# Three layer norms of a transposed encoder trunk: the variance is summed onto all partitions by one wide product, and root and reciprocal run at full width

## The chip, the cores and the metric

The kernel runs on one core of a Trainium2 chip. A core has five engines with queues of their own: TensorE (PE; its weight loads are listed as PEld), VectorE (DVE), ScalarE (ACT), GpSimd (POOL) and SyncE (SP, which only issues DMAs). The metric is the device time of one execution in microseconds, as the median of several runs; one more execution was profiled. Times inside the trace are microseconds from the start of the span, the stretch from the first to the last instruction.

## The reference

A two-layer encoder with width 1024 runs over two request groups, 256 and 512 tokens, each with 16 meta tokens in front (800 token columns in all). Layer 0 mixes tokens by latent attention, layer 1 by windowed grouped-query attention. After the mixer and after the squared-ReLU MLP of each layer stands a residual sum and a layer norm, so there are four norms:

```python
def layer_norm(x, g, b):
    xf = x.astype(jnp.float32)
    mu = jnp.mean(xf, axis=-1, keepdims=True)
    xc = xf - mu
    var = jnp.mean(xc * xc, axis=-1, keepdims=True)
    y = xc * lax.rsqrt(var + LN_EPS) * g.astype(jnp.float32) + b.astype(jnp.float32)
    return y.astype(x.dtype)
...
        h = layer_norm(DN_ALPHA * h + mix, ln1_g[i], ln1_b[i])
        h = layer_norm(DN_ALPHA * h + sqrelu_mlp(h, mlp_w1[i], mlp_w2[i]), ln2_g[i], ln2_b[i])
```

## The kernel before, in words

**Layout.** Activations lie transposed: the 1024 features are 8 chunks of 128 partitions, and the tokens run along the free axis. The 800 columns are two halves of 400 (`hf` 0 and 1); from layer 1's attention on, 384 columns of each half are left (`META` = 16 are dropped). The residual stream is `acc[:, hf, o]`, with o the feature chunk. Every matrix product is taken three times (`mm3`, lines 556 to 558): each operand is split into a rounded part and a rest, the rounding by ScalarE and the rest by VectorE (line 893 or 1661 for activations, 907 or 1624 for weights).

**A layer norm in this layout** sums over partitions, so TensorE does that. For one half (function `layer_norm` at 915 for the attention stages, at 1696 inside the MLP):

- `mean`: a sum over the eight chunks, kept up earlier by POOL and VectorE, is multiplied by `part`, a 128x128 tile of 1/1024 (line 924 or 1708). The result is the mean on every partition, in a PSUM bank `pm`. VectorE subtracts it from each chunk (927, 1710), ScalarE squares (929, 1712), VectorE and POOL add the squares up to one tile v (933 and 935, 1716 and 1718).
- `sums`: v is the stationary operand, in groups of 100 or 128 tokens, against one column of ones (942, 1725). Each product gives one PSUM column, with tokens on partitions. ScalarE takes the root of 100x4 or 128x3 values (946, 1728), VectorE the reciprocal (947, 1729).
- `scale`: TensorE spreads these few values over all partitions again (952, 1734: the column, broadcast, times the identity) into a bank `rb`. VectorE multiplies each chunk by it (957, 1739), ScalarE applies gain and bias (960, 1742), and the result is split for the next products.

Norms over single halves occur as: a0 (layer 0's first norm, half 0, at the end of the attention stage), the one inside the first MLP (the same norm, half 1), b0 and b1 (layer 0's second norm), c0 (layer 1's first norm, half 0), and the one inside the second MLP (half 1). The last norm works by tokens and has another form.

**Around the MLP's norm.** The MLP stage starts with products of half 0 alone (`head_pair`: a first product over chunks 0 to 3, which ScalarE copies out of its bank at line 1828, then a second one over chunks 4 to 7 into the same bank). They stand around `mean`, `sums` and `scale` of half 1. `right_operands` (1759) then makes differences of halves and chunks (line 1767) and splits them (1660, 1661) into the tiles `t` and `h`, which the next products read. The MLP multiplies by a scheme with fewer block products than the plain one, so VectorE and POOL add many blocks.

**Order.** Each of the four stages (attention 0, MLP 0, attention 1 with the end of MLP 0, MLP 1) is a `Plan`: a list of tasks, each with its engine, an entry for its duration in ns, what it reads and writes, and which buffers it takes. TensorE's order in a stage is written out by hand in `ORDERS`, as ranks of its tasks in the order in which the code makes them. For the other engines `forward` picks from the ready tasks by the entries and by due times counted back from the end. The instructions are then issued in that order, and each engine works off its queue in order.

Of the kernel before, what the change touches and what calls it, by code (L numbers as in the profile page):

```python
# [13 lines left out]
F32 = mybir.dt.float32  # L14
# [458 lines left out]
def tile_encoder(ctx: ExitStack, tc: tile.TileContext, ins: dict, y):  # L473
# [410 lines left out]
    def steps(plan):  # L884


        def new(tag, make=None):
            return plan.held(tag, make)
# [26 lines left out]
        def layer_norm(nm, hf, z, n, gi, bi, ss, out, name, tag, st=(), ends=(), root=()):  # L915

            pm, sb, rb = (new("w") for _ in range(3))
# [19 lines left out]
            def sums():  # L937
                v = vs[0]

                def run():  # L940
                    for i in range(n // g):
                        nc.tensor.matmul(sb.t[:g, i : i + 1], v.t[:, i * g : (i + 1) * g], ones, start=True, stop=True)

                plan.task("PE", 645, run, kind="T", reads=[v], writes=[sb], new=[sb], ends=ends)
                m = n // g
                plan.task("ACT", 300, lambda: S.activation(rst[:g, :m], sb.t[:g, :m], AF.Sqrt, bias=eps_ln[:g], scale=1.0 / D), reads=[sb, *root], writes=[("rst", nm)])
                plan.task("DVE", 170, lambda: V.reciprocal(rst[:g, :m], rst[:g, :m]), reads=[("rst", nm)], writes=[("rst", nm)])

            def scale():
                def run():  # L950
                    for i in range(n // g):
                        nc.tensor.matmul(rb.t[:, i * g : (i + 1) * g], rst[:g, i : i + 1].to_broadcast([g, P]), ident[:g, :g], start=True, stop=True)

                plan.task("PE", 800, run, kind="T", reads=[("rst", nm)], writes=[rb], new=[rb])
                for o in range(8):
                    key = ("acc", hf, o)
                    plan.task("DVE", DVE(n), lambda o=o: V.tensor_tensor(z[:, o], z[:, o], rb.t[:, :n], ALU.mult), reads=[rb, key], writes=[key])
                    plan.task(
                        "ACT", 370 + 0.835 * n,
                        lambda o=o: S.activation(z[:, o], z[:, o], AF.Identity, bias=gb[:, bi, o : o + 1], scale=gb[:, gi, o : o + 1]),  # L960
                        reads=[key], writes=[key],
                    )
                    split_to(lambda o=o: out(o), lambda o=o: z[:, o], (name, hf, o), [key, *st], n)
# [82 lines left out]
    def attention0():  # L1046
# [481 lines left out]
        mean, sums, scale = layer_norm("a0", 0, acc[:, 0], HALF, 0, 1, lambda: a0["ss"], lambda o: (a0["h"][0][:, 0, o], a0["h"][1][:, 0, o]), "h", "sqa", [st2], root=["root"])  # L1528
# [25 lines left out]
    def mlp_middle(mp, sqp, late_sum, T, n, l, tiles, yt=None, txs=None, ends=None):  # L1554
# [141 lines left out]
        def layer_norm():  # L1696
# [4 lines left out]
            pm, st, rb = (bank(f"{x}{l}") for x in ("pm", "st", "rb"))  # L1701
            vs = [tmp(f"v{l}{i}") for i in range(2)]
            rst = mp.tile([P, 4], F32, tag="rst", name=f"rst{l}", bufs=1)
            g = 100 if n == HALF else P
            m = n // g
# [14 lines left out]
            def sums():  # L1720
                v = vs[0]

                def run():
                    for i in range(m):
                        nc.tensor.matmul(st.t[:g, i : i + 1], v.t[:, i * g : (i + 1) * g], ones, start=True, stop=True)

                plan.task("PE", 645, run, kind="T", reads=[v], writes=[st], new=[st])
                plan.task("ACT", 400, lambda: S.activation(rst[:g, :m], st.t[:g, :m], AF.Sqrt, bias=eps_ln[:g], scale=1.0 / D), reads=[st], writes=["rst"])
                plan.task("DVE", 170, lambda: V.reciprocal(rst[:g, :m], rst[:g, :m]), reads=["rst"], writes=["rst"])

            def scale():
                def run():
                    for i in range(m):
                        nc.tensor.matmul(rb.t[:, i * g : (i + 1) * g], rst[:g, i : i + 1].to_broadcast([g, P]), ident[:g, :g], start=True, stop=True)

                plan.task("PE", 800, run, kind="T", reads=["rst"], writes=[rb], new=[rb])
                for o in range(8):
                    key = ("acc", 1, o)
                    plan.task("DVE", 570, lambda o=o: V.tensor_tensor(z[:, o], z[:, o], rb.t[:, :n], ALU.mult), reads=[rb, key], writes=[key])
                    plan.task(  # L1740
                        "ACT", 390 + 0.82 * n,
                        lambda o=o: S.activation(z[:, o], z[:, o], AF.Identity, bias=gb[:, bi, o : o + 1], scale=gb[:, gi, o : o + 1]),
                        reads=[key], writes=[key],
                    )
                    if o > 3:
                        split_in(h, (slice(None), 1, o), z[:, o], ("h", 1, o), [key])
# [1175 lines left out]
```

## Time and profile before

| what | us |
|---|---|
| median of 3 runs | 1713.18 (1713.09 to 1713.53) |
| the profiled execution, its own time | 1715.05 |
| its span | 1713.3 |
| TensorE busy | 1695.9 (99%) |
| VectorE busy | 1446.3 (84%) |
| ScalarE busy | 1019.7 (60%) |
| POOL busy | 321.8 (19%) |
| DMA moved | 179.32 MB, mean 105 GB/s |

A row of the timeline gives start, duration, engine, line, operation, output<-inputs, shape and count, and in brackets the idle time before it with what ended it. Matmuls are pipelined and their records overlap, so the price of one is read from start to start, not from its own duration. An fp32 product is recorded as two matmuls.

### The profile page before, as it was taken

The page shows a single profiled execution, that of the slowest core. Times are in us where ns is not written, and L with a number is a line of the kernel's source. Part 1 is how long each engine was busy: PE and PEld are TensorE (multiplying, and loading weights), DVE is VectorE, ACT ScalarE, POOL GpSimd, SP SyncE. Part 2 cuts the span into 40 slices and gives each one's busy share as a digit, 9 for nine tenths or more (in the row PEclk, how much of TensorE's full clock was granted, in tenths as well). Part 3 has the DMA queues.
Part 4 walks back from the last instruction along what each step waited for, and adds up shares of the span by engine and source line. Part 5 has one row for each costly group of instructions (what it writes and reads, how often), then busy time and mean ns, then how long its engine had stood idle before and what let it go on. Part 6 is the DMA issues. An engine that isn't in the chain of part 4 may idle for free.

```text
span 1713.3 us, 28343 instructions
## 1 busy us (share of the span) xinstructions
PE 1695.9 (99%) x10468; PEld 1583.0 (92%) x10468; DVE 1446.3 (84%) x2883; ACT 1019.7 (60%) x2132; POOL 321.8 (19%) x373
## 2 busy tenths in 40 slices
PE   9999999999999999999999999999999999999998
PEld 8998988889999999999999998889998888988996
DVE  7787777876889999989886978976888999998877
ACT  6587777773685455545644637775685445544652
POOL 1243333433100111000002332332100212000100
PEclk9999999999999999999999999999999999999999
DMA  6115534447554332222223321111464232222121
GB/s 233 61 43 128 130 87 111 114 129 214 168 202 158 102 113 72 87 74 74 62 62 106 103 66 66 51 50 51 153 209 156 90 123 82 76 86 74 50 99 74
DMA packets 62763, 179.32 MB, mean 105 GB/s; under 512 B 7456, under 2 KB 24992, under 8 KB 59424
## 3 DMA queue, kind: packets, MB, share of 16 engines
q1 hardware_dynamic: 58608, 151.95, 27.4%
q0 software_dynamic: 3584, 25.17, 6.2%
q8 instruction: 82, 1.34, 0.3%
q14 instruction: 57, 0.47, 0.1%
q10 hardware_dynamic: 432, 0.39, 0.1%
HBM read 167.92 MB, written 34.73 MB: 118 GB/s over the span
## 4 chain that ended last, share of the span: by engine, by line
PE 92%; DVE 6%; ACT 1%; issue 0%; DMA 0%; POOL 0%; ACTq 0%; DVEq 0%; POOLq 0%
PE w L558 17%; PE w L556 17%; PE w L557 17%; PE wb L556 4%; PE wb L557 4%; PE wb L558 4%; PE wa L556 3%; PE wa L558 3%; PE wa L557 3%; PE wa L1350 2%; PE wa L1317 2%; PE sa L556 2%; PE sa L558 2%; PE sa L557 2%; PE wb L2620 2%; PE wb L2602 2%
## 5 line engine op out<-in xcount | busy, mean ns | idle before, releaser
L2064 DVE TENSOR_TENSOR acc<-acc,w 128x400 f32<-128x400 f32 (+1 forms) x327 | 195.7, 614 | 16.7 <-PE w L558 15.4
L556 PE MATMUL w<-h,wsp 128*128 128x400 f32 x320 | 110.8, 346 | 1.7 <-ACT sq L1828 1.0
L557 PE MATMUL w<-h,wsp 128*128 128x400 f32 x320 | 110.3, 345 | 0.0
L558 PE MATMUL w<-h,wsp 128*128 128x400 f32 x320 | 110.1, 344 | 0.0
L1661 DVE TENSOR_TENSOR h<-sq,h 128x384 fp32r<-128x384 f32 (+1 forms) x163 | 96.9, 606 | 12.3 <-ACT h L1661 11.6
L1671 POOL TENSOR_TENSOR sq<-sq,sq 128x384 f32<-128x384 f32 (+1 forms) x28 | 33.7, 1207 | 380.8 <-DVE h L1661 182.4
L1661 ACT CAST h<-sq 128x384 fp32r<-128x384 f32 (+1 forms) x163 | 82.8, 518 | 36.7 <-DVE sq L1671 14.5
L558 PE MATMUL w<-h,wspi 128*128 128x400 f32 x280 | 96.6, 345 | 0.3 <-DVE wspi L1624 0.3
L557 PE MATMUL w<-h,wspi 128*128 128x400 f32 x280 | 96.6, 345 | 0.0
L556 PE MATMUL w<-h,wspi 128*128 128x400 f32 x280 | 96.4, 344 | 0.0
L1259 ACT ACTIVATE p<-sa,nm,rq 106x528 f32<-106x528 f32 (+1 forms) x80 | 63.5, 795 | 33.3 <-DVE nm L1256 27.0
L1837 ACT ACTIVATE sq<-sq 128x400 f32<-128x400 f32 (+1 forms) x84 | 44.5, 530 | 53.4 <-DVE sq L1833 52.7
L1833 DVE TENSOR_TENSOR sq<-sq,w 128x400 f32<-128x400 f32 (+1 forms) x97 | 54.2, 559 | 24.4 <-PE w L558 18.4
L556 PE MATMUL w<-t,wspi 128*128 128x400 f32 (+1 forms) x208 | 70.9, 341 | 0.6 <-DVE sq L1833 0.6
L556 PE MATMUL w<-wsp,h 128*128 128x512 f32 (+1 forms) x182 | 71.6, 393 | 0.0
L558 PE MATMUL w<-wsp,h 128*128 128x512 f32 (+1 forms) x182 | 71.5, 393 | 0.0
L557 PE MATMUL w<-wsp,h 128*128 128x512 f32 (+1 forms) x182 | 71.5, 393 | 0.0
L558 PE MATMUL w<-t,wspi 128*128 128x400 f32 (+1 forms) x208 | 70.9, 341 | 0.0
L557 PE MATMUL w<-t,wspi 128*128 128x400 f32 (+1 forms) x208 | 70.8, 341 | 0.0
L1286 POOL TENSOR_TENSOR p<-p,rs 106x512 f32<-106x512 f32 (+1 forms) x40 | 42.7, 1067 | 124.7 <-DVE pk L1277 67.8
L557 PE MATMUL w<-wspi,h 128*128 128x512 f32 (+1 forms) x164 | 64.5, 393 | 0.0
L556 PE MATMUL w<-wspi,h 128*128 128x512 f32 (+1 forms) x164 | 64.4, 393 | 0.0
(846 smaller groups left out, 6034.4 us busy)
## 6 DMA issues: line engine op xcount, KB each, us to landing
wrawo<-in_w_o_dram SPq DMA_DIRECT2D x32, 512.0 KB, 3.6
wraw0d<-in_w2b_dram SPq DMA_DIRECT2D x27, 512.0 KB, 3.5
us<-in_w1q_dram POOLq DMA_DIRECT2D x12, 1024.0 KB, 8.4
wraw1d<-in_w2b_dram SPq DMA_DIRECT2D x21, 512.0 KB, 3.5
ds<-in_w2q_dram POOLq DMA_DIRECT2D x12, 512.0 KB, 5.4
sq<-kept SPq DMA_DIRECT2D x26, 200.0 KB, 3.4
sq<-kept SPq DMA_DIRECT2D x26, 192.0 KB, 3.2
us<-us POOLq DMA_DIRECT2D x4, 1024.0 KB, 5.0
```

What stands on the lines that cost most here:

```text
L556: first = nc.tensor.matmul(out, lh, rh, start=start, stop=False, **kw)
L557: nc.tensor.matmul(out, lh, rl, start=False, stop=False, **kw)
L558: last = nc.tensor.matmul(out, ll, rh, start=False, stop=stop, **kw)
L1259: lambda: S.activation(P_().rearrange("p (a b) -> p a b", b=264), v(), AF.Exp, bias=nm.t[:qm, 0:1], scale=sc, accum_out=rs.t[:qm, 0:1]),
L1286: f = lambda row=row, r=r, w=w: G.tensor_tensor(row()[:, META:T], row()[:, META:T], r().to_broadcast([qm, w]), ALU.mult)
L1317: nc.tensor.transpose(ps.t[:, k * qm : (k + 1) * qm], src[k], ident[:qm, :qm])
L1350: nc.tensor.matmul(av[64 * e : 64 * e + 64, :n], vt.t[:, k, h0 + 64 * e : h0 + 64 * e + 64], PT.t[:, e, k, :n], start=k == 0, stop=False, ...
L1661: return lambda: S.copy(hi(), view()), lambda: V.tensor_tensor(lo(), view(), hi().bitcast(F32), ALU.subtract)
L1833: plan.task("DVE", 570, lambda: V.tensor_tensor(d.t[:, :n], d.t[:, :n], ps.t[:, :n], ALU.add), reads=[ps, d], writes=[d])
L1837: plan.task("ACT", 510, lambda: S.activation(d.t[:, :n], d.t[:, :n], AF.Relu, scale=scale), reads=[d], writes=[d])
L2064: f = lambda: V.tensor_tensor(z, z, ps.t[:, : z.shape[-1]], op)
L2602: nc.tensor.transpose(ps.t[:, n * P : (n + 1) * P], SM.t[:, a : a + P], ident)
```

## The change

Three norms get a new form: a0 and the two inside the MLPs. In `sums`, v is now the moving operand against `part`, the tile of 1/1024 that the mean already uses. One product of full width leaves the variance on all 128 partitions, in one PSUM bank. The root and the reciprocal run in place in that bank over 128x400 (128x384 in the second MLP), and VectorE multiplies the chunks by it. The spreading products, their bank and the small tile `rst` are gone from these norms. b0, b1 and c0 keep the old form.

TensorE's order is written anew for three stages (attention 0, MLP 0, MLP 1); attention 1 keeps its own. Each of the three has one task fewer, the spreading, so ranks behind it drop by one. Beyond that, 34 of the 369 tasks of attention 0, 23 of 350 of MLP 0 and 30 of 320 of MLP 1 stand elsewhere, by at most nine places, and they are spread over the stages. In a0 `sums` stands one product step earlier. In MLP 0 the second product of head 0 is finished before that of head 1, and the products around `sums` and `scale` are turned; in MLP 1 the first twelve places are the same.

```diff
@@ attention 0: its end
-    "287 285 289 294 293 296 298 292 291 295 301 304 299 297 305-306 309 300 302 310 303 312 314 313 307 317 308 311 318 316 319 315 "
-    "320 322 324-326 323 327 321 329 331 328 332 330 333-337 339-346 338 354 349 347-348 350-351 358 355 362-363 352 359 353 360 "
-    "356-357 364 361 365-369",
...
+    "318 324 322 325-326 323 329 327 321 331 328 332 330 333-337 339-346 338 353 347-350 357 354 361 351 362 358-359 352 355-356 363 "
+    "360 364-368",
@@ MLP 0: its beginning
-    "0-4 7-8 5 9-12 6 13-17 19 21 20 22 18 23 25-30 35 31-34 24 36-41 43 46 45 42 47-48 50 49 44 52 51 56 53-55 57 60 58 61 59 62 69 "
+    "0-4 7 5-6 9 8 10 12 11 13-14 16 15 18 20 19 21 17 24-25 22 26-29 34 30-31 23 32-33 35-40 42 45 44 41 46-47 49 48 43 51 55 52-54 50"
@@ MLP 1: its beginning
-    "0-5 7 6 8-14 21 19 15 20 16 22 17-18 23-25 27-29 36 30 26 31 33 32 34 41 40 38 37 42 39 35 49 45 43-44 50-51 48 47 52 46 53-54 57 "
+    "0-5 7 6 8-13 20 18 14 19 15 22-23 21 16-17 24 26-27 25 28-30 32 38 31 33 35 39 37 36 43 40-41 34 45 47-48 42 49-51 44 46 52-53 56 "
...
-        def layer_norm(nm, hf, z, n, gi, bi, ss, out, name, tag, st=(), ends=(), root=()):
-
-            pm, sb, rb = (new("w") for _ in range(3))
+        def layer_norm(nm, hf, z, n, gi, bi, ss, out, name, tag, st=(), ends=(), root=(), wide=False):
+
+            pm, sb = new("w"), new("w")
+            rb = sb if wide else new("w")
...
+                if wide:
+                    plan.task("PE", 765, lambda: nc.tensor.matmul(sb.t[:, :n], part, v.t[:, :n], start=True, stop=True), reads=[v], writes=[sb], new=[sb], ends=ends)
+                    plan.task("ACT", ACT(n), lambda: S.activation(sb.t[:, :n], sb.t[:, :n], AF.Sqrt, bias=eps_ln, scale=1.0), reads=[sb, *root], writes=[(sb, "sd")])
+                    plan.task("DVE", 2570, lambda: V.reciprocal(sb.t[:, :n], sb.t[:, :n]), reads=[(sb, "sd")], writes=[(sb, "r")])
+                    return
...
-                plan.task("PE", 800, run, kind="T", reads=[("rst", nm)], writes=[rb], new=[rb])
+                if not wide:
+                    plan.task("PE", 800, run, kind="T", reads=[("rst", nm)], writes=[rb], new=[rb])
+                by = (rb, "r") if wide else rb
...
-                    plan.task("DVE", DVE(n), lambda o=o: V.tensor_tensor(z[:, o], z[:, o], rb.t[:, :n], ALU.mult), reads=[rb, key], writes=[key])
+                    plan.task("DVE", DVE(n), lambda o=o: V.tensor_tensor(z[:, o], z[:, o], rb.t[:, :n], ALU.mult), reads=[by, key], writes=[key])
...
-        mean, sums, scale = layer_norm("a0", 0, acc[:, 0], HALF, 0, 1, lambda: a0["ss"], lambda o: (a0["h"][0][:, 0, o], a0["h"][1][:, 0, o]), "h", "sqa", [st2], root=["root"])
+        mean, sums, scale = layer_norm("a0", 0, acc[:, 0], HALF, 0, 1, lambda: a0["ss"], lambda o: (a0["h"][0][:, 0, o], a0["h"][1][:, 0, o]), "h", "sqa", [st2], root=["root"], wide=True)
...
             def sums():
                 v = vs[0]
-
-                def run():
-                    for i in range(m):
-                        nc.tensor.matmul(st.t[:g, i : i + 1], v.t[:, i * g : (i + 1) * g], ones, start=True, stop=True)
-
-                plan.task("PE", 645, run, kind="T", reads=[v], writes=[st], new=[st])
-                plan.task("ACT", 400, lambda: S.activation(rst[:g, :m], st.t[:g, :m], AF.Sqrt, bias=eps_ln[:g], scale=1.0 / D), reads=[st], writes=["rst"])
-                plan.task("DVE", 170, lambda: V.reciprocal(rst[:g, :m], rst[:g, :m]), reads=["rst"], writes=["rst"])
+                plan.task("PE", 765, lambda: nc.tensor.matmul(st.t[:, :n], part, v.t[:, :n], start=True, stop=True), reads=[v], writes=[st], new=[st])
+                plan.task("ACT", 530, lambda: S.activation(st.t[:, :n], st.t[:, :n], AF.Sqrt, bias=eps_ln, scale=1.0), reads=[st], writes=[(st, "sd")])
+                plan.task("DVE", 2570, lambda: V.reciprocal(st.t[:, :n], st.t[:, :n]), reads=[(st, "sd")], writes=[(st, "r")])
 
             def scale():
-                def run():
-                    for i in range(m):
-                        nc.tensor.matmul(rb.t[:, i * g : (i + 1) * g], rst[:g, i : i + 1].to_broadcast([g, P]), ident[:g, :g], start=True, stop=True)
-
-                plan.task("PE", 800, run, kind="T", reads=["rst"], writes=[rb], new=[rb])
                 for o in range(8):
                     key = ("acc", 1, o)
-                    plan.task("DVE", 570, lambda o=o: V.tensor_tensor(z[:, o], z[:, o], rb.t[:, :n], ALU.mult), reads=[rb, key], writes=[key])
+                    plan.task("DVE", 570, lambda o=o: V.tensor_tensor(z[:, o], z[:, o], st.t[:, :n], ALU.mult), reads=[(st, "r"), key], writes=[key])
```

The numbers in the tasks (765, 530, 2570) are the planner's own entries in ns, by which it lays out the queues.

More of the change, by code (lines that the diff above doesn't have):

```diff
@@ L1700, in layer_norm @@
             total = plan.held("sq", None, late_sum)
-            pm, st, rb = (bank(f"{x}{l}") for x in ("pm", "st", "rb"))
+            pm, st = (bank(f"{x}{l}") for x in ("pm", "st"))
             vs = [tmp(f"v{l}{i}") for i in range(2)]
-            rst = mp.tile([P, 4], F32, tag="rst", name=f"rst{l}", bufs=1)
-            g = 100 if n == HALF else P
-            m = n // g
             def mean():
```

41 rows, old and new, of the table ORDERS are left out of this document.

## The prediction

> **What bounds the kernel now.** I read the page first: busy shares, then the chain that ended last.
>
> ```profile
> span 1713.3 us, 28343 instructions
> PE 1695.9 (99%) x10468; PEld 1583.0 (92%) x10468; DVE 1446.3 (84%) x2883; ACT 1019.7 (60%) x2132; POOL 321.8 (19%) x373
> PE 92%; DVE 6%; ACT 1%; issue 0%; DMA 0%; POOL 0%; ACTq 0%; DVEq 0%; POOLq 0%
> ```
>
> TensorE (PE) is the bound: 99% busy and 92% of the chain. VectorE (DVE) is second with 6%. So a microsecond that leaves TensorE's queue is a microsecond of the span, as long as what TensorE reads next is there in time. Which stages have no such reserve is seen in the busy time by stage (columns: stretch, its length, then PE, PEld, DVE, ACT, POOL busy with instruction counts, granted clock, DMA share, GB/s) and in the list of waits (total us, times, longest).
>
> ```profile
> 447.00:460.00 13.00, 11.87 (x65) 10.55 (x64) 11.56 (x19) 8.61 (x16) 2.11 (x2) 1.00 0.26 88
> 460.00:560.00 100.00, 100.00 (x554) 100.00 (x553) 88.60 (x152) 67.45 (x126) 3.46 (x2) 1.00 0.55 181
> 560.00:640.00 80.00, 78.90 (x430) 77.82 (x429) 79.08 (x130) 38.80 (x65) 11.59 (x7) 1.00 0.37 112
> 1219.00:1230.00 11.00, 9.67 (x52) 8.46 (x51) 9.24 (x17) 7.05 (x13) 2.04 (x2) 1.00 0.24 85
> PE w L556 <- ACT sq L1828: 2.1, 4, 0.8
> ```
>
> The two MLP norms begin in the stretches at 447 and 1219. TensorE idles 1.13 and 1.33 us there, nearly all of it in four waits (2.1 us) for ScalarE copies out of PSUM (L1828) that sit between the norm's squares. From 460 to 560 TensorE never idles while DVE has 11.4 us free; from 560 to 640 DVE is full. The second row also gives the price of one ordinary 400-wide product: 100 us / 554 = 0.18 us from start to start (0.173 at 384 wide, by width).
>
> **What is removed and added on TensorE.** The variance's column products (L942, L1725) and the spreading products (L952, L1734) each stand between 400- or 384-wide products, so their price is the interval from the last ordinary start before them to the second one after, less two ordinary steps. First the attention stage's norm a0, with its mean product (L924), which has exactly the form of the new wide product: the tile of 1/1024 times 128x400.
>
> ```profile
> 412.57 0.34 PE L558 MATMUL wa<-o,wsp 128*128 128x400 f32 x1
> 412.76 0.83 PE L924 MATMUL wa<-ssum,part 128*128 128x400 f32 x2
> 413.61 0.34 PE L557 MATMUL wa<-o,wsp 128*128 128x400 f32 x1
> ...
> 424.18 0.34 PE L558 MATMUL wa<-o,wspi 128*128 128x400 f32 x1
> 424.36 0.79 PE L942 MATMUL wa<-ones,sqa 128*100 128x1 f32 x8
> 425.28 0.34 PE L557 MATMUL sa<-o,wspi 128*128 128x400 f32 x1
> ...
> 426.01 0.35 PE L558 MATMUL sa<-o,wspi 128*128 128x400 f32 x1
> 426.20 1.03 PE L952 MATMUL wa<-ident,rsta 100*128 100x100 f32 x8
> 427.28 0.35 PE L557 MATMUL wa<-o,wspi 128*128 128x400 f32 x1
> ```
>
> Wide product: 413.61 - 412.57 - 0.36 = 0.68 us. Column products: 425.28 - 424.18 - 0.36 = 0.74. Spreading: 427.28 - 426.01 - 0.36 = 0.91. So a0 saves 0.74 + 0.91 - 0.68 = **0.97 us** of TensorE. Nearly all of it is the spreading; one wide product is hardly cheaper than four narrow ones. The first MLP's norm has the same forms and durations, and I give it the same 0.97; the second MLP's has three column groups and width 384:
>
> ```profile
> 457.06 0.79 PE L1725 MATMUL w<-ones,sq 128*100 128x1 f32 x8
> 459.99 1.03 PE L1734 MATMUL w<-ident,rst 100*128 100x100 f32 x8
> ```
>
> ```profile
> 1230.32 0.34 PE L558 MATMUL w<-hc,wsp 128*128 128x384 f32 x1
> 1230.49 0.72 PE L1725 MATMUL w<-ones,sq 128*128 128x1 f32 x6
> 1231.34 0.34 PE L557 MATMUL w<-hc,wspi 128*128 128x384 f32 x1
> ...
> 1233.08 0.34 PE L558 MATMUL w<-hc,wspi 128*128 128x384 f32 x1
> 1233.25 0.83 PE L1734 MATMUL w<-ident,rst 128*128 128x128 f32 x6
> 1234.10 0.34 PE L557 MATMUL w<-hc,wsp 128*128 128x384 f32 x1
> ```
>
> Columns 1.02 - 0.35 = 0.67, spreading 0.67, wide product 0.68 x 384/400 = 0.65: **0.69 us** saved. Sum on TensorE: 0.97 + 0.97 + 0.69 = **2.63 us**.
>
> **What is added on ScalarE and VectorE.** The root goes from 100x4 to the full width, in place in PSUM; a 400-wide ScalarE pass out of PSUM is in the trace (L1828).
>
> ```profile
> 457.60 0.51 ACT L1828 ACTIVATE sq<-w 128x400 f32<-128x400 f32 x1
> 458.00 0.26 ACT L1728 ACTIVATE rst<-w,eps_ln 100x4 f32<-100x4 f32 x1
> ```
>
> So 0.25 us more, three times, on an engine 60% busy: nothing on the path beyond the latency counted below. A wide reciprocal stands nowhere in the trace; the nearest rows have one and four columns (min/median/max ns).
>
> ```profile
> L1262 DVE RECIPROCAL rs<-rs x80: 144/164/166, 108.0 to 377.6; 106x1 f32<-106x1 f32 x64, 104x1 f32<-104x1 f32 x16
> L2553 DVE RECIPROCAL rs<-rs x24: 168/178/179, 1039.1 to 1165.2; 128x4 f32<-128x4 f32 x24
> ```
>
> Medians: 14 ns for three more columns, 4.7; I take 5 ns a column, 0.16 + 400 x 0.005 = 2.16 us (2.08 at 384). Ends: below, no dearer than an ordinary pass over PSUM, 0.53 us (two in 1.05 us, the 461.06 row below); above, longest four against shortest one, 35/3 = 11.7 ns a column, 4.8 us. I stay at the middle because both medians rest on many rows.
>
> [...]
>
> **Where it lies.** In the first MLP, DVE is queued like this around the root:
>
> ```profile
> 456.21 2.35 DVE L1624 TENSOR_TENSOR wspi<-wraw0f,wspi 128x1024 fp32r<-128x1024 f32 x2
> 458.48 0.17 DVE L1729 RECIPROCAL rst<-rst 100x4 f32<-100x4 f32 x1
> 458.57 1.20 DVE L1624 TENSOR_TENSOR wsp<-wraw0f,wsp 128x1024 fp32r<-128x1024 f32 x1
> 461.06 1.05 DVE L1739 TENSOR_TENSOR acc<-acc,w 128x400 f32<-128x400 f32 x2 [1.30 <-PE w L1734]
> ```
>
> The multiplications (L1739) waited 1.30 us for the spreading product, which TensorE's order puts at 459.99 although the small reciprocal was done at 458.65. Now: wide product 457.06 to 457.74, root from 457.9 to 458.4, reciprocal to about 460.7, multiplications from 460.8: no later than before. What is late is the weight split (L1624) that the reciprocal pushes behind it and everything after: 2.16 - 0.17 - 1.30 = 0.69 us. The same for the second MLP (idle 0.76): 2.08 - 0.18 - 0.76 = 1.14 us. Who waits? The first tight reader is TensorE's first product with the right-hand sums t (L1661), whose last quarter reads the last t:
>
> ```profile
> 488.21 0.56 DVE L1661 TENSOR_TENSOR t<-tsum,t 128x400 fp32r<-128x400 f32 x1
> 492.04 0.34 PE L556 MATMUL w<-t,wspi 128*128 128x400 f32 x1
> ...
> 1234.12 1.48 DVE L1739 TENSOR_TENSOR acc<-acc,w 128x384 f32<-128x384 f32 x3 [0.76 <-PE w L1734]
> ...
> 1260.80 1.06 DVE L1661 TENSOR_TENSOR t<-tsum,t 128x384 fp32r<-128x384 f32 x1 [0.23 <-ACT t L1661]
> 1265.15 0.34 PE L556 MATMUL w<-t,wsp 128*128 128x384 f32 x1
> ```
>
> Room: 492.04 - 488.77 = 3.27 us and 1265.15 - 1261.86 = 3.29 us. TensorE now comes 0.97 and 0.69 us sooner, DVE 0.69 and 1.14 later: 1.61 and 1.46 us stay. So the reciprocal costs nothing on the path; without that cover, each microsecond of lateness would cost one. The lateness itself is gone before the full stretch at 560, since DVE has 11.4 us free before it.
>
> In a0 the summing task also moves one product step ahead (1.10 us):
>
> ```profile
> 422.38 0.57 DVE L1436 SCALAR_TENSOR_TENSOR acc<-xr,wa 128x400 f32<-128x400 f32 x1 [1.03 <-PE wa L558]
> 422.86 0.57 DVE L935 TENSOR_TENSOR sqa<-sqa,sqa 128x400 f32<-128x400 f32 x1
> ```
>
> It would start at 423.26, before its operand (L935, done 423.43). Either DVE takes L935 ahead of L1436, for which it idled 1.03 us, or TensorE waits some 0.2 us; I take nothing. The half that this norm makes is read by the MLP stage at 447; its eight multiplications, at 0.53 us each behind the spreading product at 426.20, are done by about 432, so 15 us of other products hide its reciprocal. Behind it in DVE's queue stand evacuations and one weight split.
>
> **The new orders** add and drop no other TensorE task: 34 of 369, 23 of 350 and 30 of 320 tasks stand elsewhere, by nine places at most. The other engines' queues, SP's and POOL's DMA issues among them, are laid out anew around that, with the same issues. I take zero, with ends from the waits row: 2.1 us gained if those four waits go, 2.1 lost if as many come. One bank is held longer (the variance's, until the last multiplication) and one is not taken any more; no wait of today is for a bank at these places other than those four.
>
> **Sum.** The profiled execution took 1715.05 us, 1.75 around its span of 1713.3; less 2.63 it would be 1712.42. It ran 1.87 above the median of the runs, 1713.18, so against the median: 1710.55, and I say **1710.5 us**, 0.15% faster. What a measurement of this kernel can tell from no change is about 0.2%, 3.4 us: 1709.75 and 1716.6 are the borders.
>
> **Rivals.**
> *The orders also take standing waits away.* For it: the first MLP's line changes exactly at its two waits (1.0 of the 2.1 us). Against: the first twelve places of the second MLP's line are the old ones. First MLP's alone 1709.5, all four 1708.4; about 1709.0.
> *Late operands.* The reciprocal at its upper end, 4.8 us: lateness 3.33 and 3.66 us against 2.30 and 2.60 of room, so 1.0 + 1.1 us come back: 1712.6. For it: DVE is over 88% busy there. Against: the slope of the small rows.
> *The gain is given back.* DVE is full from 560 to 640; if it sets the pace there, TensorE only arrives earlier and waits: 1713.2. Against: DVE idles before that stretch, waiting for TensorE, so it moves forward with it.
> *Slower.* The reciprocal stands in DVE's queue ahead of a weight split or evacuation that TensorE needs next, and TensorE stands for its whole length at all three norms: 2.16 + 2.16 + 2.08 = 6.4, less 2.63: 1717.0. It decides from 0.9 us of wait per norm on. For it: the first MLP's new line begins its fourth head product one step after the third instead of three, so that weight's split is needed earlier. Against: both splits (456.21, two in 2.35 us) fit before the root.
>
> **Numbers.** Forecast 0.52 (its own range 1709.7 to 1711.5: a wait of 0.2 us here or there, readings of a few hundredths each), waits removed 0.28, late operands 0.09, given back 0.04, slower 0.07. Faster by over 0.2%: the second case and a sliver of the first, 0.32; slower 0.07; within, 0.61. The range goes from all waits gone, 1708.4, to the gain given back, 1713.3, and leaves out the slower case and some of the tails.
>
> **What would show it.** Right: no spreading products at the three places, one wide product of 0.68 us each, reciprocal rows of about 2.2 us, the 1.30 and 0.76 us of DVE idle before the multiplications gone, no TensorE wait for t. Wrong: a TensorE wait for a DVE t, h or weight row between 455 and 495 or 1230 and 1270; a reciprocal above 3.5 us; or savings that come from rows far from the norms.

## The result, and the profile after

| | before | after |
|---|---|---|
| median of 6 runs each, us | 1713.43 (1713.09 to 1715.27) | 1705.26 (1704.34 to 1706.25) |
| profiled execution, its own time, us | 1715.05 | 1706.25 |
| span, us | 1713.3 | 1704.5 |
| TensorE busy, us | 1695.9 | 1686.4 |

The ratio is 0.995, with a 95% interval from 0.9937 to 0.9962: 8.2 us less, where 2.6 were forecast. The time lies below the range. The page of the profile after, its first lines and the engines' shares of the chain:

```profile
span 1704.5 us, 28243 instructions
PE 1686.4 (99%) x10430; PEld 1576.8 (93%) x10430; DVE 1452.2 (85%) x2888; ACT 1019.8 (60%) x2132; POOL 320.7 (19%) x368
PE 90%; DVE 7%; ACT 2%; DMA 1%; issue 1%; POOL 0%; ACTq 0%; DVEq 0%; POOLq 0%
```

TensorE has 38 records fewer, exactly those of the three norms (16 become 2 in each of the first two, 12 become 2 in the last), and still fills the span. The forecast of the norms themselves can be read in the timeline: start, duration, engine, line, operation.

```profile
422.67 0.34 PE L558 MATMUL wa<-o,wsp 128*128 128x400 f32 x1
422.86 0.83 PE L946 MATMUL wa<-sqa,part 128*128 128x400 f32 x2
423.22 0.65 PE L556 MATMUL sa<-o,wspi 128*128 128x400 f32 x1
423.71 0.34 PE L557 MATMUL sa<-o,wspi 128*128 128x400 f32 x1
```

```profile
1227.21 0.34 PE L558 MATMUL w<-hc,wspi 128*128 128x384 f32 x1
1227.39 0.81 PE L1727 MATMUL w<-sq,part 128*128 128x384 f32 x2
1227.74 0.63 PE L556 MATMUL w<-hc,wsp 128*128 128x384 f32 x1
1228.21 0.34 PE L557 MATMUL w<-hc,wsp 128*128 128x384 f32 x1
```

By the interval method the wide product takes 423.71 - 422.67 - 0.36 = 0.68 us in a0 and 1.00 - 0.35 = 0.65 in MLP 1, as forecast. So the norms are not where the surplus is. To find it, follow one landmark through both traces: the product that makes the mean of a norm (line 924 or 1708 before, 925 or 1713 after), by the first and last start in a group's row. Before:

```profile
L924 PE MATMUL wa<-ssum,part x2: 497/498/498, 412.8 to 413.1; 128*128 128x400 f32 x2
L1708 PE MATMUL w<-sqsum,part x4: 486/544/603, 448.2 to 1221.2; 128*128 128x400 f32 x2, 128*128 128x384 f32 x2
L924 PE MATMUL wb<-ssc,part x2: 486/538/590, 1187.8 to 1188.2; 128*128 128x384 f32 x2
```

After:

```profile
L925 PE MATMUL wa<-ssum,part x2: 497/498/498, 412.4 to 412.7; 128*128 128x400 f32 x2
L1713 PE MATMUL w<-sqsum,part x4: 486/536/589, 447.3 to 1218.1; 128*128 128x400 f32 x2, 128*128 128x384 f32 x2
L925 PE MATMUL wb<-ssc,part x2: 486/538/589, 1184.7 to 1185.1; 128*128 128x384 f32 x2
```

The lead of the changed kernel is 0.4 us at a0's mean, 0.9 at MLP 0's, 3.1 at c0's (the last norm ahead of MLP 1), and 1713.3 - 1704.5 = 8.8 at the end. From c0's mean to the end it takes 1704.5 - 1184.7 = 519.8 us against 525.5: **5.7 us are won in and around MLP 1**, whose norm gives only 0.7. The rest is spread over the whole stage. It shows in the down-projection, where a split weight (`wsp`, `wspi`, 512 wide) streams past a hidden tile (`h`, the kernel's `h2`) as the stationary operand. A stretch of such products of before and of after (min/median/max ns, first and last start):

```profile
L556 PE MATMUL w<-wsp,h x6: 395/396/396, 1349.9 to 1353.4; 128*128 128x512 f32 x6
```

```profile
L556 PE MATMUL w<-wspi,h x6: 389/391/397, 1344.9 to 1348.3; 128*128 128x512 f32 x6
```

Between the first and the last of the six lie five rounds of three products: 3.5/15 = 0.233 us from start to start before, 3.4/15 = 0.227 after. These starts are rounded to tenths, so the rows only point the way; over the whole stage the steps are 0.2332 and 0.2274 us (table below), and the groups by line and shape agree (count, busy us, mean ns of one record), before and then after:

```profile
L556 PE MATMUL w<-wsp,h 128*128 128x512 f32 x178 | 70.4, 396 | 0.0
L556 PE MATMUL w<-wspi,h 128*128 128x512 f32 x160 | 63.3, 396 | 0.0
```

```profile
L556 PE MATMUL w<-wspi,h 128*128 128x512 f32 x182 | 71.1, 390 | 0.0
L556 PE MATMUL w<-wsp,h 128*128 128x512 f32 x156 | 60.7, 389 | 0.0
```

There are 338 such products on each of the lines 556 to 558, 1014 in all, each 6 ns shorter: up to 6 us. They have no part in any norm, and the diff doesn't touch them. What it does touch is memory: the 16-byte tile `rst` of the MLP norms was taken from the MLP's pool, and with it gone every tile that the pool places behind it starts 32 bytes lower. In the programs as built, the `h2` tiles of MLP 1 start at 86208 + 3072k before and at 86176 + 3072k after; the split weights start at 3232 + 8192k in both.

### The profile page after: what moved, and what is told of

Read it like the earlier page. It is cut to its first block, busy times and chain, and to the rows that moved or that the text cites. A ratio compares the mean times of both kernels' runs of the same rounds, so it can differ in the third digit from the quotient of the medians.

```text
span 1704.5 us, 28243 instructions
## 1 busy us (share of the span) xinstructions
PE 1686.4 (99%) x10430; PEld 1576.8 (93%) x10430; DVE 1452.2 (85%) x2888; ACT 1019.8 (60%) x2132; POOL 320.7 (19%) x368
## 4 chain that ended last, share of the span: by engine, by line
PE 90%; DVE 7%; ACT 2%; DMA 1%; issue 1%; POOL 0%; ACTq 0%; DVEq 0%; POOLq 0%
PE w L558 16%; PE w L556 16%; PE w L557 16%; PE wb L556 4%; PE wb L557 4%; PE wb L558 4%; PE wa L556 3%; PE wa L558 3%; PE wa L557 3%; PE wa L1325 2%; PE wa L1358 2%; PE sa L556 2%; PE sa L558 2%; PE wb L2615 2%; PE sa L557 2%; PE wb L2597 2%
## 5 line engine op out<-in xcount | busy, mean ns | idle before, releaser
L556 PE MATMUL w<-h,wsp 128*128 128x400 f32 x308 | 106.8, 347 | 1.9 <-ACT sq L1823 1.1
L557 PE MATMUL w<-h,wsp 128*128 128x400 f32 x308 | 105.8, 343 | 0.0
L558 PE MATMUL w<-h,wsp 128*128 128x400 f32 x308 | 105.8, 343 | 0.0
L558 PE MATMUL w<-h,wspi 128*128 128x400 f32 x292 | 100.3, 344 | 0.3 <-DVE wspi L1632 0.3
L557 PE MATMUL w<-h,wspi 128*128 128x400 f32 x292 | 100.5, 344 | 0.0
L556 PE MATMUL w<-h,wspi 128*128 128x400 f32 x292 | 100.2, 343 | 0.0
L556 PE MATMUL w<-wspi,h 128*128 128x512 f32 (+1 forms) x190 | 73.3, 386 | 0.0
L557 PE MATMUL w<-wspi,h 128*128 128x512 f32 (+1 forms) x190 | 73.3, 386 | 0.0
L558 PE MATMUL w<-wspi,h 128*128 128x512 f32 (+1 forms) x190 | 73.2, 385 | 0.0
L558 PE MATMUL w<-t,wspi 128*128 128x400 f32 (+1 forms) x200 | 68.4, 342 | 0.0
L557 PE MATMUL w<-t,wspi 128*128 128x400 f32 (+1 forms) x200 | 68.2, 341 | 0.0
L556 PE MATMUL w<-t,wspi 128*128 128x400 f32 (+1 forms) x200 | 68.1, 341 | 0.0
L1263 DVE TENSOR_REDUCE nm<-sa 106x1 f32<-106x528 f32 (+1 forms) x80 | 55.6, 700 | 9.9 <-PE sa L558 8.9
L556 PE MATMUL w<-t,wsp 128*128 128x384 f32 (+1 forms) x184 | 62.6, 340 | 0.6 <-DVE sq L1828 0.6
```

What stands on the lines that cost most here:

```text
L556: first = nc.tensor.matmul(out, lh, rh, start=start, stop=False, **kw)
L557: nc.tensor.matmul(out, lh, rl, start=False, stop=False, **kw)
L558: last = nc.tensor.matmul(out, ll, rh, start=False, stop=stop, **kw)
L1263: plan.task("DVE", DVE(528), lambda: V.tensor_reduce(nm.t[:qm, 0:1], v(), axis=AX.XY, op=ALU.max, negate=True), reads=[ps], writes=[nm], n ...
```

## The experiments

Theory: where tiles start in memory sets the step of the 128x512 products, and the removed tile moved them. Rivals: the new orders, or less work for the other engines. Four kernels take tile and orders apart. Each ratio is against the kernel before, run again beside its set (medians 1713.31 to 1713.49 us).

**The tile put back into the changed kernel.**

```diff
             vs = [tmp(f"v{l}{i}") for i in range(2)]
+            padding = {0: 4, 1: 4}.get(l)
+            if padding:
+                rst = mp.tile([P, padding], F32, tag="rst", name=f"rst{l}", bufs=1)
+                plan.task("POOL", 60, lambda: nc.gpsimd.memset(rst[:, :1], 0.0), writes=["rst"])
```

> The changed kernel, with the 16-byte tile of the two MLP norms put back into the MLP pool (nothing computes with it; GpSimd sets one column of it to zero), so that every tile allocated behind it in the MLPs (the hidden tiles h2 and the split weights w22) starts 32 bytes higher, where it was before the change. Theory (address): the 128x512 products of MLP 1, whose stationary operand is an h2 tile, go back from 0.227 to 0.233 us from start to start (some 1000 products x 0.006 = 6 us at most; 5.0 us is what the two traces show for the rest of MLP 1), MLP 0 gives back some 1.2 us: 1711.4 us. Rival (orders): the gain comes from the new orders of the products, the tile does nothing: 1705.3 us. Rival (norms alone): the new form of the norms speeds the stages by less work on the other engines: 1705.3 us, too.

Measured: 1712.45 us (11 runs), 0.9993 of before, interval 0.9984 to 1.0002. A tile with which nothing computes costs 7.2 us by the medians. The step is the old one again:

```profile
L556 PE MATMUL w<-wspi,h 128*128 128x512 f32 x182 | 72.0, 396 | 0.0
```

**The kernel before with its tile moved.**

```diff
-            rst = mp.tile([P, 4], F32, tag="rst", name=f"rst{l}", bufs=1)
+            rst = gp.tile([P, 4], F32, tag="rst", name=f"rst{l}", bufs=3)
```

> The kernel before, whole, with one word changed: the 16-byte tile of the two MLP norms comes from the global pool's ring of such tiles instead of the MLP pool, so that h2 and w22 start 32 bytes lower, as after the change. Theory (address): 128x512 products of MLP 1 step at 0.227 us, 1713.4 - 6.2 = 1707.2 us. Rivals (orders; norms alone): 1713.4 us, the step stays 0.233 us.

Measured: 1706.74 us, 0.9963 of before (0.9950 to 0.9975), so one changed word is worth 6.6 us by the medians (1713.31 to 1706.74) without any change to the norms. The group row, and then the landmark row of c0's mean:

```profile
L556 PE MATMUL w<-wspi,h 128*128 128x512 f32 x160 | 62.3, 390 | 0.0
```

```profile
L924 PE MATMUL wb<-ssc,part x2: 486/538/589, 1184.7 to 1185.1; 128*128 128x384 f32 x2
```

With its span of 1704.7 us this is 520.0 us for MLP 1 (525.5 before). Both rivals fall as causes of the large part.

Counted from a0's mean product to the end of the span, how an execution begins plays no part. By this count the two pairs agree: with the old norms (before, and before with its tile moved) the tile's place is worth 1300.5 - 1293.9 = 6.6 us, with the new ones (tile back against the changed kernel) 1298.7 - 1292.1 = 6.6 us. Of it 5.4 us lie behind MLP 1's mean product and 1.1 to 1.2 us in the stretch from MLP 0's mean to b0's. What is left for norms and orders together is 1.8 us in both pairs (1300.5 to 1298.7, 1293.9 to 1292.1).

**The changed kernel with the old orders** (ranks of before, the three spreading tasks taken out).

> The changed kernel with the written orders of before (the three spreading tasks taken out of them, the ranks behind them lowered by one), the tile gone as in the change. Theory (address): the new orders are worth nothing, 1705.3 us within 1.0. Rival (orders): 1705.3 + 6 = 1711 us.

Measured: 1706.98 us, 0.9965 (0.9952 to 0.9977). Its MLP 1 takes 519.9 us, so the new orders have no part in the 5.7 us. Its median lies 1.7 us above the changed kernel's, more than the 1.0 that was allowed.

**The norms alone**: old orders and the tile back, both edits above in one kernel.

> The three norms alone: the orders of before without the spreading tasks, and the 16-byte tile put back, so that the addresses are those of before. The prediction's sum for the edit without new orders was 2.6 us: 1710.7 us. By e3 the orders of before cost 1.7 to 2.2 us at the start of MLP 0, where the product of the mean and the first products behind it wait for VectorE and ScalarE: then 1713 us, no gain at all. If orders and addresses do not add up: something else.

Measured: 1714.85 us, 1.0003 of before (0.9994 to 1.0012): no gain at all. The waits of TensorE from 440 to 600 us (total, times, longest), in this kernel's line numbers:

```profile
PE w L1683 <- DVE sqsum L1417: 1.5, 1, 1.5
PE w L522 <- DVE acc L1410: 0.8, 1, 0.8
PE w L522 <- ACT sq L1793: 0.7, 1, 0.7
```

L1683 is the mean product of MLP 0. It waits 1.5 us for the last sum, 0.2 before. VectorE's queue shows why:

```profile
425.98 2.67 DVE L914 RECIPROCAL wa<-wa 128x400 f32<-128x400 f32 x1 [0.41 <-ACT wa L913]
428.55 1.21 DVE L873 TENSOR_TENSOR wspi<-wrawo,wspi 128x1024 fp32r<-128x1024 f32 x1
429.68 3.92 DVE L931 TENSOR_TENSOR acc<-acc,wa 128x400 f32<-128x400 f32 x8
...
446.68 2.51 DVE L859 TENSOR_TENSOR h<-acc,h 128x400 fp32r<-128x400 f32 x5
449.10 0.56 DVE L1417 TENSOR_TENSOR sqsum<-sqsum,acc 128x400 f32<-128x400 f32 x1
```

Behind the wide reciprocal of a0 the eight multiplications come later (the first starts at 429.68 us, before at 427.27), the splits of the normed half (L859) move back with them, and five of them end up directly ahead of the last sum, which ends 1.5 us later than before (449.66 against 448.18). With the new orders that wait is 0.6 us (the list of waits of the changed kernel):

```profile
PE w L556 <- ACT sq L1823: 2.2, 4, 0.8
...
PE w L1713 <- DVE sqsum L1451: 0.6, 1, 0.6
```

So the orders matter, though not by taking standing waits away: the four waits for ScalarE copies are there as before, 2.2 us. They take back most of a wait that came with the wide norms. That a0's reciprocal brings it is read from the queue; no run changes a0 alone.

**Which tile, and what about its start.** A longer `w22` tile (1032 columns allocated, 1024 used) moves, of the tiles that these products read, `h2` alone by 32 bytes; 32 bytes at the end of the global pool move split weights and `h2` together; the padding of the first experiment with 16 floats moves `h2` by 64 bytes.

> The changed kernel with the w22 tiles 32 bytes longer, so that only the h2 tiles, which lie behind them, start 32 bytes higher (192 past a multiple of 512, as before the change), while the w22 tiles stay where the change put them (160). Theory (the start of h2 alone): the 128x512 step is 0.233 us again, 1711.5 us. Rival (w22: its products, or VectorE's writes into it): 1705.3 us and 0.227 us.

Measured: 1713.23 us, 0.9993 (0.9984 to 1.0002). `h2` alone is enough for the 128x512 step (records of 396 ns again, 390 in the changed kernel). The `w22` tiles have a small part of their own: where they keep their place, MLP 1 takes 524.4 us in place of 525.2, and 130 products of `hc` with them take 0.173 us from start to start in place of 0.176.

> The changed kernel with 32 bytes of padding at the end of the global pool, so that every tile behind it starts 32 bytes higher: the h2 tiles of MLP 1 start where they did before the change (192 past a multiple of 512 bytes), but the split weights that stream past them move along (from 160 to 192). Theory A (what counts is how the stationary and the moving operand stand to one another): the 128x512 step stays at 0.227 us and the time near 1705.3 us. Theory B (what counts is where the stationary operand starts by itself): the step goes back to 0.233 us as in e1, some 5 us, and the products elsewhere, whose stationary operand is a split weight, can lose too: 1711 us or more.

Measured: 1708.71 us, 0.9968 (0.9956 to 0.9980). Two groups, 512 and 384 wide (line 558 is 556 elsewhere), and for comparison the second one's row in the changed kernel:

```profile
L558 PE MATMUL w<-wspi,h 128*128 128x512 f32 x182 | 71.0, 390 | 0.0
...
L558 PE MATMUL w<-t,wsp 128*128 128x384 f32 x100 | 34.0, 340 | 0.6 <-DVE sq L1830 0.6
```

```profile
L556 PE MATMUL w<-t,wsp 128*128 128x384 f32 x100 | 33.8, 338 | 0.6 <-DVE sq L1828 0.6
```

`h2` starts where it did before the change, and the 512-wide products stay fast (0.2271 us from start to start): theory A holds for them, it is the relation of the two operands. The 384-wide products lost instead. Their moving tiles `hc` and `t` didn't move while their weights did; from start to start they went from 0.173 to 0.176 us (means over some 570 and 540 products).

> As e1, with a tile of 64 bytes in place of the 16: h2 and w22 start at 96 past a multiple of 128 bytes (32 in the changed kernel, 64 before). If what counts is the start within 64 bytes (32 good, 0 bad), the time is that of the changed kernel, 1705.3 us; if what counts is that the stationary and the moving operand start alike (the split weights start at 32), or the start within 128 bytes, the step is another one than 0.227 us and the time somewhere up to 1711.4 us. Rival (orders or norms alone): 1705.3 us, and e1 the same.

Measured: 1711.64 us, 0.9989 (0.9980 to 0.9998): 64 bytes are no better than 32 (both 0.2332 us from start to start), so a start within 64 bytes is not what counts here.

**The distance by itself.** Padding in MLP 1 alone (`{1: 24}`, 32, 48 or 64 floats in the first experiment's edit) changes the distance from where the moving weight starts to where the stationary slice starts, taken within 512 bytes.

> The changed kernel with 96 bytes of padding ahead of the tiles of MLP 1 alone, so that the distance from where a moving weight starts to where its h2 operand starts (0 past a multiple of 512 bytes in the changed kernel) is 96. From the steps so far (128x512: distance 0 gives 0.227 us, 32 and 64 give 0.233; 128x384: distance 192 gives 0.1733, 224 gives 0.1756), theory: slow, 0.233 us, 1710.3 us (MLP 1 alone gives back some 5). Rival (only where h2 starts counts, and 160 past 512 is the one good place): slow, too.

> As the run by 96, with 128 bytes: distance 128. From the 400-column products of MLP 0, whose t operand is at distances of 64 and 128 at 0.183 us and at 0 and 192 at 0.180 to 0.181 (counted within 256 bytes): slow, 0.233 us, 1710.3 us. If a distance counts only within 128 bytes: 0.227 us, 1705.3 us.

> As the run by 96, with 192 bytes: distance 192. From the 384-column products (distance 192 at 0.1733 us, 224 at 0.1756) and the 400-column ones: fast, 0.227 us, 1705.3 us. If distance 0 alone is good for 128x512 products: 0.233 us, 1710.3 us.

> As the run by 96, with 256 bytes: distance 256. If the rule repeats after 256 bytes, as the 400-column products suggest (0 and 256 at 0.181 us, 192 and 448 at 0.181): 0.227 us, 1705.3 us. If only after 512 or more: 0.233 us, 1710.3 us.

Measured: 1712.55 us (0.9992, interval 0.9983 to 1.0002), 1710.70 (0.9984, 0.9975 to 0.9994), 1709.14 (0.9974, 0.9965 to 0.9984) and 1705.66 (0.9955, 0.9941 to 0.9970). All kernels in one table; the step is the mean start-to-start interval, intervals above 0.25 us left out, of more than 900 128x512 products followed by one of their kind, "MLP 1" the time from c0's mean to the end of the span:

| distance, bytes | kernel | step, us | MLP 1, us |
|---|---|---|---|
| 0 | after; before with its tile moved; old orders | 0.2274 (after) | 519.8; 520.0; 519.9 |
| 0, 384-wide ones worse | all 32 higher | 0.2271 | 522.8 |
| 32 | before; tile back; `h2` alone; norms alone | 0.2332 (before) | 525.5; 525.2; 524.4; 525.1 |
| 64 | by 64 | 0.2332 | 525.1 |
| 96 | by 96 | 0.2342 | 525.6 |
| 128 | by 128 | 0.2330 | 524.8 |
| 192 | by 192 | 0.2315 | 523.3 |
| 256 | by 256 | 0.2273 | 519.4 |

For these products a distance of 0 or 256 is good (0.2271 to 0.2274 us) and the others tried are not (0.2315 to 0.2342). The expectation for 192, drawn from narrower products, was a miss: there it is a little better than 128 and far from fast.

**The other three norms in the new form, too** (`wide=True` for b0, b1 and c0, their spreading tasks out of the order).

> The changed kernel with the other three norms (both halves after the cross attention, and the one ahead of MLP 1) in the new form, too; their spreading tasks are taken out of the orders and nothing is reordered. If each saves what a0 did (1.0 us of TensorE's line) and the work behind them covers the reciprocal of 2.6 us: 1702.3 us. If VectorE, which does the reciprocals, is late with what TensorE needs next, as e3 showed for MLP 0 with orders that were not made for it: 1705 to 1709 us. The h2 tiles stay where the change put them, so the 128x512 step is 0.227 us in either case.

Measured: 1716.57 us, 1.0012 (1.0003 to 1.0021), above both expectations; the 128x512 products are as fast as expected (0.227 us, MLP 1 519.9 us). The mark that the load of the exponential's table waits for is one that the new form doesn't set, so that load comes at 912.12 us, ahead of the roots of b0 and b1. Two more table loads of 1.28 us follow, one for the roots (938.97) and one for the exponentials (1038.56). The output of the smaller request group is not the reference's; why isn't settled, so only the time of the queues is to be read. TensorE's longest waits:

```profile
PE w L522 <- ACT sq L1789: 2.2, 4, 0.8
PE wb L2581 <- DVE rm L2494: 2.0, 1, 2.0
PE wb L2563 <- DVE sma L2538: 1.5, 2, 1.2
PE wb L912 <- DVE sqb L902: 1.3, 2, 1.0
PE w L1679 <- DVE sqsum L2621: 1.1, 1, 1.1
```

All but the first are new or longer than in the changed kernel, 5.9 us together, and all of those are for VectorE. Attention 1 in its present order seems not to cover the reciprocals of 2.6 us; with two more table loads in ScalarE's queue, this is argued and not shown. From b1's mean product to c0's it takes 234.0 us against 225.4, and a part of that is TensorE's granted clock, which stood at half for 3.4 us from 1072.2 us on. How much new orders would take back was not tried.

## Why the prediction was wrong, point by point

- **The step that failed: the sum left out a term.** The prediction added up what the diff does to instructions and queues ("Sum on TensorE: 0.97 + 0.97 + 0.69 = 2.63 us") and so took every product that the diff doesn't name at its old step. The removed tile `rst` is named in the description of the change, and the prediction gives it no price. By its effect on where other tiles start, `h2` above all, it is worth 6.6 us (7.2 by the medians of tile back and changed kernel). This alone puts the time outside the range. The sign named for being wrong did appear: savings in rows far from the norms.
- **Price of the products: right where the norms stand, but not kept whole.** The wide product takes 0.68 and 0.65 us. Product by product, 0.97 us is won at a0 (0.97 forecast), 0.85 at MLP 0's norm (0.97) and 0.71 at MLP 1's (0.69). Between the first two, 0.4 is lost again at MLP 0's mean product, whose wait for the last sum has grown from 0.2 to 0.6 us. Some 0.5 is lost at 1437 us, where a product of MLP 1 waits for a weight row of VectorE; in the kernels with the old orders it doesn't. The waits of 1380 to 1475 us, first before with its tile moved, then the changed kernel:

```profile
PE w L558 <- DVE w L1624: 0.5, 1, 0.5
```

```profile
PE w L558 <- DVE w L1632: 0.8, 2, 0.4
```

  By the count from a0's mean to the end, 1.8 us are left in place of 2.63.
- **The reciprocal: too cheap.** Forecast 2.16 and 2.08 us; these are the rows (min/median/max ns):

```profile
L1729 DVE RECIPROCAL w<-w x2: 2557/2607/2657, 458.7 to 1230.0; 128x400 f32<-128x400 f32 x1, 128x384 f32<-128x384 f32 x1
```

  100 ns for 16 columns is 6.2 ns a column, not 5. The small rows' slope didn't give the time: 2.66 and 2.56 us are 0.50 and 0.48 more than forecast. The wide rows work in PSUM and the small ones in SBUF; what part that has was not taken apart.
- **What it is hidden behind: no wait for a `t`, but one for another operand.** The 1.30 us of VectorE's idle time before the multiplications is gone:

```profile
458.67 2.66 DVE L1729 RECIPROCAL w<-w 128x400 f32<-128x400 f32 x1
461.23 1.21 DVE L1632 TENSOR_TENSOR wsp<-wraw0f,wsp 128x1024 fp32r<-128x1024 f32 x1
462.36 1.52 DVE L1734 TENSOR_TENSOR acc<-acc,w 128x400 f32<-128x400 f32 x3
```

  They begin 1.3 us later than before (462.36 against 461.06), and 2.2 us later when both are counted from MLP 0's mean product, where "no later" was forecast. The prediction kept the rest of the queue as it was; in the queue as laid out anew one weight split stands ahead of the reciprocal and one between it and the multiplications. Yet TensorE's list of waits has none for a `t`. In a0 "15 us of other products hide its reciprocal" holds for the half that this norm makes. What was late is the sum of the other half, behind the splits in the same queue. With the old orders the whole gain is gone (from a0's mean to the end 1300.5 us before, 1300.5 with the norms alone).
- **"The new orders: zero".** Against the norms with the old orders they are worth 1.7 us (1706.98 to 1705.26) with the tile gone and 2.4 us (1714.85 to 1712.45) with the tile in place by the medians, and 1.8 us with the tile in place when counted from a0's mean (1300.5 to 1298.7). That is near the 2.1 us allowed for, and it comes by a mechanism that the prediction had listed as two rivals apart: late operands, and orders that take waits away.
- **The rivals.** "Waits removed" named a size that the orders did have (some 2 us), by luck: the four waits are still there. "Late operands" came true, at another reader than the one named (the sum ahead of MLP 0's mean, not `t`) and in full only with the old orders. "Given back" and "slower" didn't happen in the changed kernel; the norms alone come out at no change. That the change touches something it doesn't name was missing among the rivals.
- **Edit and orders without the address.** The forecast's 1710.5 us is to be set against the run with the tile put back, 1712.45: 0.07% faster, not 0.15%, and not told from no change. In the two profiled executions the spans differ by 3.0 us (1713.3 and 1710.3), but 1.1 us of that lie ahead of a0's mean product (412.8 and 411.6). From there to the end the 1.8 us remain.

## What to carry to other kernels

When a diff adds, removes or resizes a tile, look up in the built programs which tiles behind it move, and compare the start-to-start step of the products that read them; here a change of 32 bytes outweighed the edit more than three times over. To judge an edit by itself, keep the addresses with a dummy tile of the old size. And when an operation in a queue gets longer, follow the queue to the next operand that another engine reads, also where it belongs to another piece of work.

## What the runs showed of the hardware that was not expected

**The step of some products depended on how far apart their operands start.** The 128x512 products of MLP 1 go from 0.227 to 0.233 us by the distance alone, with a good place at 0 and at 256 bytes among the seven distances of the table. The 400-wide products of MLP 0 with `t` show a pattern that repeats after 256 bytes, too: means of 0.179 to 0.181 us at distances of 0, 192, 256 and 448, and 0.183 to 0.184 at 64, 128, 320 and 384. So in these two groups the place of the one operand against the other matters for the time. By what mechanism stays open. So do the groups that don't follow: the 512-wide products of the latent attention (moving `cq`, stationary split weight) take 0.230 to 0.233 us at every distance seen, 0 and 256 included, and the 384-wide ones of layer 1's attention with `hb` take 0.174 to 0.176 us at all eight. So the distance is shown for the groups above and is no rule for every product. Lining up the 400-wide operands of MLP 0 was not tried.

**In two executions the clock stood at half behind a wait.** In the profiled execution of the old orders with the tile gone, TensorE is busy for 0.52 of the 2 us up to 448, waiting for the sum ahead of MLP 0's mean product. Right after it the granted clock (the third number from the end) stands at half, from 448.2 to 451.6 us:

```profile
448.00:450.00 2.00, 2.00 (x5) 1.44 (x6) 0.70 (x2) 0.10 (x1) 0.00 (x0) 0.55 0.00 0
450.00:452.00 2.00, 2.00 (x8) 1.99 (x8) 2.00 (x5) 2.00 (x5) 0.52 (x1) 0.60 0.00 0
```

In the kernel with the norms alone the same wait (0.52 of 2 us busy) is followed by the full clock:

```profile
450.00:452.00 2.00, 2.00 (x11) 1.71 (x11) 1.30 (x3) 0.70 (x2) 0.00 (x0) 1.00 0.00 0
```

Compared product by product, the halved clock costs 1.4 us between 447 and 460. The kernel with all norms wide shows the same behind a wait at 1070 us. So this wait cost about twice the 1.5 us that the list of waits gives for it; what decides whether the clock halves was not found.

**Executions begin in two ways.** Busy time by stretch from 6 to 10 us, before and then before with its tile moved (PE busy with its instruction count comes first after the length):

```profile
6.00:8.00 2.00, 2.00 (x11) 1.40 (x5) 1.76 (x6) 1.67 (x5) 0.00 (x0) 1.00 0.95 309
8.00:10.00 2.00, 2.00 (x8) 0.94 (x7) 0.39 (x2) 0.34 (x1) 0.00 (x0) 1.00 0.98 307
```

```profile
6.00:8.00 2.00, 1.97 (x13) 1.40 (x15) 1.72 (x5) 1.76 (x5) 0.00 (x0) 1.00 0.92 293
8.00:10.00 2.00, 2.00 (x14) 1.68 (x14) 0.67 (x2) 0.66 (x2) 0.00 (x0) 1.00 0.86 273
```

While the first inputs arrive, the one execution starts 19 products and the other 27, and from 11 us on the second leads by 1.7 us, and by 1.9 at the end of attention 0, with nothing else changed so far. In seven of the fourteen traces the 201st record of TensorE starts at 32.0 to 32.5 us, in the other seven at 33.5 to 34.3. The times of before fall into two groups, too (some 1713.3 and some 1715 us), which a late beginning would explain; as each kernel has one trace, this isn't shown. The profiled executions of the changed kernel and of the one with the tile put back began late like that of before, so their spans compare. What sets the beginning isn't settled; it limits what medians can tell to about 2 us.
